# Layer 1 of a two-layer stream encoder: plain chunks by tile, column sums in two goes, paced stores

## The chip, the cores and the metric

The kernel runs on one core of one Trainium2 chip. The metric is the device time of one execution in microseconds. Before the change it is 2186.94 us (median of three runs, 2185.77 to 2187.29).

The engines named here are PE (TensorE, matrix products; PEld is its weight load), DVE (VectorE), ACT (ScalarE), POOL (GpSimd) and SP (SyncE, which issues most DMAs). All work from queues of their own, in order, and wait for each other on semaphores.

## The reference

A sequence of 1024 prompt frames and 32 sample frames, each of 1024 channels, goes through two layers. Cut to what matters here:

```python
for i in range(DEPTH):                       # DEPTH = 2
    mod = silu(c) @ w_ada[i] + b_ada[i]      # sh1, sc1, gt1, sh2, sc2, gt2
    h = rmsnorm(x, g_norm[i, 0]) * (1 + sc1) + sh1
    if i == 0:
        mix, v = sgu_mixer(h, ...)           # gated mixing in chunks of frames
    else:
        mix = pool_mixer(h_ext, ...)         # trailing means over 2, 4, 8, 16 frames, then a map per group
    x = x + gt1 * rmsnorm(mix, g_norm[i, 1])
    h = rmsnorm(x, g_norm[i, 2]) * (1 + sc2) + sh2
    f = square(relu(h @ ffn_w_up[i])) @ ffn_w_down[i]     # 1024 -> 4096 -> 1024
    x = x + gt2 * rmsnorm(f, g_norm[i, 3])
```

All of it is in float32. The change concerns layer 1 (`i = 1`): its FFN, the last line, and the order in which the pool mixer's work is done around it.

## The kernel before

**Tiles and chunks.** Frames are columns; they are cut into three tiles: tile 0 and tile 1 of 384 prompt frames each, tile 2 of 256 prompt and 32 sample frames (288 columns). The FFN's 4096 hidden channels are cut into eight chunks of 512. One chunk for one tile (a chunk-tile) is four up products (`ffn_item.up`, 8 x 3 matmuls each) and eight down products (`ffn_item.down`, 4 x 3 matmuls each), 192 matmuls. The factor 3 comes from splitting each float32 operand into a high and a low part in a format that PE multiplies at full rate: high by high, high by low, low by high. Tiles named with h and l (`hh`/`hl`, `fh`/`fl`, `wh`/`wl`) are these parts. A chunk's down products are put off (`pending`, `flush`) until the next chunk-tile's first up product has been issued.

**The passes.** The list `passes` (L321 to L328) says in which order chunks and tiles are taken. In layer 1: chunks 0 and 1 for tile 0, the same two for tile 1, then chunks 2 and 3 with each weight used for both tiles (chunk 3 with tile 1 first), then four "combined" chunks 4 to 7 (`COMBINED = 4`), then all eight chunks for tile 2.

**Combined chunks.** For chunks 4 to 7 the up products of tiles 0 and 1 are computed together (`combined_item`, L1554) by a scheme with seven block products in place of eight: blocks of the weights and of the two tiles' columns are added and subtracted beforehand. The weight side is made by `do_s` (L441) in a scratch area that lies in tile 2's `acc`. The column side is made by `sums_of_columns` (L1752), one "column" of four blocks at a time: three loads of tiles 0's and 1's modulated rows from DRAM (`md[0]`, `md[1]`), four subtractions on DVE, four high parts on ACT and four low parts on DVE. The results live in pieces of buffers that other work has left: the `hh`/`hl` rooms of tile 2, half of those of tile 1, two slots of the weight pool, and others. Before tile 2's rooms and `acc` can be used so, tile 2's modulated rows are stored to DRAM (`md[2]`); `late_modulation` (L1823) loads them again and makes tile 2's `hh` and `hl` at the last combined chunk.

**Weights.** `stream` lists all weight items in the order of their use, 512 KB each, eight to a chunk. SP loads an item into one of three `raw` buffers; `do_w` (L416) makes its high part on ACT and its low part on DVE, in two of 16 slots of the pool `W`. `stream_ready` (L620) limits the items in hand: eight before the position `wtight` (L371), and from there on 14 slots, which is seven items.

**Order of the work around the products.** Everything that isn't a product of the main sequence is a generator in the queue `fillers`: the residual and norm after a layer-0 FFN, the pool mixer and the modulation of layer 1 (`ffn1_0`, `ffn1_1`, `ffn1_2`, one for each tile, with `mix_to_ffn`, L1717), the column sums (`sums`), late modulation, and the output (`out_0`, `out_1`, `out_2`, from `to_out`, L2021). `weave` (L721) is called after each product. It prepares weight items, and pulls steps of the first two fillers while a running estimate of DVE's time is behind PE's. A filler's step may yield a number: that filler is then not pulled again for so many microseconds of the planner's time. `finish(tag)` (L732) pulls all that is left of a filler at once. Tile t's first layer-1 chunk calls `finish("ffn1_t")` (in `run_ffn`, L2003), and the last plain chunk-tile of tile 1 calls `finish("ffn1_2")` and only then starts the filler `sums` (L1548 to L1550). `run_ffn` calls `finish("sums")` ahead of each combined chunk.

**Output.** Tiles 0 and 1 end in `to_out`: a residual, then for each of eight groups of channels a transpose on DVE and four stores of that group, three from SP and one from POOL (L2084). Each group is one step that yields False.

Of the kernel before, what the change touches and what calls it, by code (L numbers as in the profile page):

```python
# [9 lines left out]
F32 = mybir.dt.float32  # L10
F32R = mybir.dt.float32r
AF = mybir.ActivationFunctionType
# [23 lines left out]
def tile_stream_encoder_step(  # L36
# [285 lines left out]
    passes += [(0, c, every) for c in range(2, 4)]  # L322
    passes += [(0, c, [t]) for t in every for c in range(4, 8)]
    pair = every[:-1]
    passes += [(1, c, [t]) for t in pair for c in (0, 1)]
    passes += [(1, c, pair if c != 7 - COMBINED else pair[::-1]) for c in range(2, 8)]
    combined = range(len(passes) - COMBINED, len(passes))
    passes += [(1, c, [NT - 1]) for c in range(8)]  # L328

# [103 lines left out]
    def temp(i):  # L433
        return scratch[:, 1024 + 384 * i : 1408 + 384 * i]
# [1064 lines left out]
    def ffn_item(p, t, after):  # L1499
        l, c, tiles = passes[p]  # L1500
        last = t == tiles[-1]
        n = ncol[t]
        hid = []

        def up(j):
            ps = ps_up(f"pf{l}_{c}_{t}_{j}")
            products(ps, n, up_terms(("up", p, j), t))
            if last:
                w_finish(("up", p, j))
            r = t_m(f"r{l}_{c}_{t}_{j}")  # L1510
            act(out=r[:, :n], in_=ps[:, :n], func=AF.Relu)  # L1511
            a, b = t_hid("h", f"fh{l}_{c}_{t}_{j}"), t_hid("l", f"fl{l}_{c}_{t}_{j}")
            act(out=r[:, :n], in_=r[:, :n], func=AF.Square)
            split(a, b, r, n)
            hid.append((a, b))

        def down():
            for d in range(KB):
                ps = ps_dn(f"pg{l}_{c}_{t}_{d}")
                wh, wl = need_w(("dn", p, d // 2))  # L1520
                terms = []
                for j in range(4):
                    o = j * 256 + (d % 2) * P
                    a, b = hid[j]
                    terms.append((wh[:, o : o + P], wl[:, o : o + P], a[:, :n], b[:, :n]))
                products(ps, n, terms)
                accumulate(t, d, ps, c == 0)
                if d == 0 and after is not None:
                    st = Stat(t, f"rf{l}_{t}", l == 0 or t < NT - 1)
                if after is not None:  # L1530
                    st.square(d)
                    if l == 1 and t == NT - 1:
                        scale_last(d)
                        if d in (2, 4, 6):
                            turn_last(d - 2)
# [12 lines left out]
        if p + 1 == combined[0] and t == 1:  # L1548
            finish("ffn1_2")
            fillers.append(("sums", sums_of_columns()))  # L1550
        pending.append(down)


    def combined_item(p, after):  # L1554
# [121 lines left out]
        weave()  # L1676
        for t in tiles:
            down(t)

    last_ps = {}  # L1680

# [35 lines left out]
    def mix_to_ffn(st, l):  # L1717
        t = st.t
        out = []
        need_ada(l, 2)  # L1720
        yield from residual(st, l, 1, f"r1_{l}_{t}", out)
        if l == 1 and t == NT - 1:
            for q in range(P // DEC):
                nc.sync.dma_start(xsd[:, :, q, :], acc[t][DEC * q : DEC * (q + 1), :, HALO:])
        need_ada(l, 4)
        if l == 0:
            yield from modulate(out[0], l, 2, 3)
            return
        got = []
        yield from out[0].finish(got)  # L1730
        if t < NT - 1:
            yield from apply(t, l, 2, 3, got[0])
            nc.sync.dma_start(md[t], acc[t][:, :, HALO:])
            return
        for k in range(KB):
            for c0, w, v in segs[t]:
                a = A(t, k, c0, w)
                stt(
                    out=a,
                    in0=a,  # L1740
                    scalar=coef[:, l, 2, v, k : k + 1],
                    in1=got[0][:, c0 : c0 + w],
                    op0=ALU.mult,
                    op1=ALU.mult,
                )
            yield False
        nc.sync.dma_start(md[t], acc[t][:, :, HALO:])
        yield False

    sums = {}  # L1750

    def sums_of_columns():  # L1752
        n = ncol[0]
        rooms = [room(part, NT - 1, f"sums_{part}", F32R) for part in "hl"]
        pieces = [
            r.rearrange("p k n -> p (k n)")[:, i * n : (i + 1) * n] for r in rooms for i in range(6)
        ]
        for name, tag, bufs, shape, k in (
            ("c", "c", 3, [P, 384], 1),
            ("r", "rr", 2, [P, 384], 1),  # L1760
            ("a", "aa", 2, [P, 512], 1),
            ("w", "W", W_SLOTS, [P, 1024], 2),
        ):
            for i in range(2 if tag == "W" else bufs):
                x = work.tile(shape, F32R, tag=tag, bufs=bufs, name=f"sums_{name}{i}")
# [9 lines left out]
        sums["spare"] = pieces  # L1775
        dsh = small.tile([P, 4], F32, tag="st", bufs=6, name="dshift")
        sh = shift[:, 1, 1, :, 0].rearrange("p (k a) -> p k a", a=2)
        tt(out=dsh, in0=sh[:, :, 1], in1=sh[:, :, 0], op=ALU.subtract)
        sums["parts"] = {}
        for i in range(4):  # L1780
            t1, t3, t2 = (temp(m) for m in range(3))
            t4 = t_m(f"sums_m{i}")
            nc.sync.dma_start(t1, md[0][:, 2 * i, :])
            nc.sync.dma_start(
                scratch[:, 1408:2176].rearrange("p (a n) -> p a n", a=2), md[1][:, 2 * i : 2 * i + 2, :]
            )
            nc.sync.dma_start(t4, md[0][:, 2 * i + 1, :])
            yield 3.0
            tt(out=t1, in0=t3, in1=t1, op=ALU.subtract)
            tt(out=t3, in0=t2, in1=t3, op=ALU.subtract)  # L1790
            tt(out=t2, in0=t2, in1=t1, op=ALU.subtract)
            tt(out=t4, in0=t4, in1=t2, op=ALU.subtract)
            yield True
            todo = (
                (2, t3, dsh[:, i : i + 1]),
                (0, t1, None),
                (1, t2, shift[:, 1, 1, 2 * i + 1, 0:1]),
                (3, t4, None),
            )
            for j, src, b in todo:  # L1800
                hi, lo = his.pop(0), los.pop(0)
                sums["parts"][j, i] = hi, lo
                if b is None:
                    act(out=hi, in_=src, func=AF.Copy)
                else:
                    act(out=hi, in_=src, func=AF.Identity, bias=b, scale=1.0)
            yield True
            for j, src, b in todo:
                hi, lo = sums["parts"][j, i]
                if b is None:  # L1810
                    tt(out=lo, in0=src, in1=hi.bitcast(F32), op=ALU.subtract)
                else:
                    stt(
                        out=lo,
                        in0=src,
                        scalar=b,
                        in1=hi.bitcast(F32),
                        op0=ALU.add,
                        op1=ALU.subtract,
                    )  # L1820
            yield False

    def late_modulation(t):  # L1823
        a = acc[t][:, :, HALO:]
# [196 lines left out]
    def to_out(st):  # L2021
# [48 lines left out]
        def run():  # L2070
# [9 lines left out]
            for k in range(KB):  # L2080
                time["dve"] += 0.1 + npr / 930.0
                nc.vector.transpose(out=turned[:, k, :], in_=A(t, k))
                for q in range(P // DEC):
# [4 lines left out]
                yield False  # L2088

        fillers.append((f"out_{t}", run()))  # L2090

# [47 lines left out]
```

## Time and profile before

| | |
|---|---|
| median of three runs | 2186.94 us |
| lowest and highest | 2185.77, 2187.29 us |
| profiled execution, its own time | 2187.31 us |
| profiled execution, span | 2185.4 us |
| mean granted PE clock over the span | 0.993 |
| DMA | 321.63 MB, mean 147 GB/s |

The span runs from the first instruction of the program to the last one's end; the execution's own time has 1.9 us around it. The profile comes from one execution. Its page has the busy time of each engine, slices of the span with a digit for the busy share, the chain of work that ended last, the costliest groups of instructions and the DMAs. Other views answer questions about a stretch: busy time of the engines in it, who waited for whom, groups of instructions by line, or the instructions in order of time. Names in these rows are the program's tile names without their numbers (`pf` is a PSUM tile of an up product, `pg` of a down product, `pn` of a norm, `pp` of the pool mixer's map). Matmuls overlap in the pipeline, so the mean duration of one is about twice the time from one to the next; the count in a stretch tells the rate. L80 is the helper through which nearly all DVE instructions are issued, so those are told apart by their tiles.

### The profile page before, as it was taken

How to read it: one execution, taken by the hardware profiler on the slowest of the kernel's cores; microseconds unless marked ns; L12 is line 12 of the kernel's file. 1: busy time of each engine (PE TensorE's matmuls, PEld its weight loads, DVE VectorE, ACT ScalarE, POOL GpSimd, SP SyncE). 2: the span in 40 equal slices, each digit the busy share in tenths (PEclk: the TensorE clock that was granted, in tenths of full speed). 3: DMA queues.
4: the chain of work that ended last, by engine and by line, in shares of the span. 5: the costliest groups of instructions: out<-in, count | busy, mean ns of one | idle time of the engine just before them, and what ended most of it. 6: DMA issues, size and time to landing. Idle time of an engine off the chain costs nothing.

```text
span 2185.4 us, 33239 instructions
## 1 busy us (share of the span) xinstructions
PE 2141.9 (98%) x13137; PEld 2063.5 (94%) x13137; DVE 1491.8 (68%) x2649; ACT 1000.0 (46%) x1716; POOL 15.4 (1%) x34
## 2 busy tenths in 40 slices
PE   9999999999999999999999999987999999999998
PEld 6778999999999999999999999977999999999998
DVE  6777738567787549567887778775666555577664
ACT  5534331233465552314346466655444443355454
POOL 0000000000000000000000000000000000001000
PEclk9999999999999999999999999998999999999999
DMA  8486524353356444335665566564343222156771
GB/s 303 145 261 211 167 80 134 96 161 115 112 152 200 126 147 142 107 97 172 180 183 158 154 185 201 164 190 134 105 123 119 78 68 68 49 152 172 208 205 62
DMA packets 380849, 321.63 MB, mean 147 GB/s; under 512 B 39730, under 2 KB 343386, under 8 KB 380692
## 3 DMA queue, kind: packets, MB, share of 16 engines
q1 hardware_dynamic: 380020, 318.61, 48.0%
q8 instruction: 103, 1.69, 0.3%
q0 software_dynamic: 640, 0.88, 0.1%
q14 instruction: 54, 0.44, 0.1%
q10 hardware_dynamic: 32, 0.01, 0.0%
HBM read 283.28 MB, written 36.17 MB: 146 GB/s over the span
## 4 chain that ended last, share of the span: by engine, by line
PE 89%; DVE 5%; DMA 3%; ACT 2%; issue 1%; DVEq 0%; ACTq 0%
PE pg L923 10%; PE pg L925 10%; PE pg L924 10%; PE pf L923 8%; PE pf L924 8%; PE pf L925 8%; PE po L923 3%; PE po L924 3%; PE po L925 3%; PE pu L923 3%; PE pu L925 3%; PE pu L924 3%; PE pv L951 2%; PE pv L950 2%; PE pv L952 2%; PE pf_0a L1588 2%
## 5 line engine op out<-in xcount | busy, mean ns | idle before, releaser
L923 PE MATMUL pg<-fh,wh_dn 128*128 128x384 f32 (+1 forms) x1440 | 463.6, 322 | 1.4 <-ACT fh L1336 1.0
L924 PE MATMUL pg<-fl,wh_dn 128*128 128x384 f32 (+1 forms) x1440 | 461.0, 320 | 2.1 <-DVE fl L80 1.9
L925 PE MATMUL pg<-fh,wl_dn 128*128 128x384 f32 (+1 forms) x1440 | 460.2, 320 | 2.3 <-DVE wl_dn L80 2.3
L923 PE MATMUL pf<-hh,wh_up 128*128 128x384 f32 (+1 forms) x1280 | 409.7, 321 | 3.4 <-ACT r L1511 1.7
L924 PE MATMUL pf<-hl,wh_up 128*128 128x384 f32 (+1 forms) x1280 | 408.2, 319 | 0.8 <-DVE hl L80 0.8
L925 PE MATMUL pf<-hh,wl_up 128*128 128x384 f32 (+1 forms) x1280 | 408.0, 319 | 0.1
L923 PEld LDWEIGHTS pg<-fh,wh_dn 128*128 128x128 f32 x1440 | 270.1, 188 | 5.2 <-ACT fh L1336 3.0
L924 PEld LDWEIGHTS pg<-fl,wh_dn 128*128 128x128 f32 x1440 | 270.3, 188 | 4.0 <-DVE fl L80 3.4
L925 PEld LDWEIGHTS pg<-fh,wl_dn 128*128 128x128 f32 x1440 | 270.1, 188 | 2.8 <-DVE wl_dn L80 2.8
L80 DVE TENSOR_TENSOR wl_up<-raw,wh_up 128x1024 fp32r<-128x1024 f32 (+1 forms) x160 | 177.1, 1114 | 131.6 <-ACT wh_up L419 130.7
L80 DVE TENSOR_TENSOR acc<-acc,pg 128x384 f32<-128x384 f32 (+1 forms) x336 | 172.3, 516 | 107.1 <-PE pg L925 106.3
L923 PEld LDWEIGHTS pf<-hh,wh_up 128*128 128x128 f32 x1280 | 240.6, 188 | 5.0 <-ACT r L1511 2.3
L924 PEld LDWEIGHTS pf<-hl,wh_up 128*128 128x128 f32 x1280 | 240.8, 188 | 2.0 <-DVE hl L80 1.5
L925 PEld LDWEIGHTS pf<-hh,wl_up 128*128 128x128 f32 x1280 | 241.2, 188 | 1.0 <-DVE wl_up L80 1.0
L419 ACT ACTIVATE wh_up<-raw 128x1024 fp32r<-128x1024 f32 x136 | 143.8, 1059 | 204.5 <-PE pf L924 118.7
L80 DVE TENSOR_TENSOR wl_dn<-raw,wh_dn 128x1024 fp32r<-128x1024 f32 x152 | 185.4, 1221 | 73.6 <-ACT wh_dn L419 63.9
L419 ACT ACTIVATE wh_dn<-raw 128x1024 fp32r<-128x1024 f32 x152 | 160.5, 1058 | 158.5 <-PE pg L924 117.0
L80 DVE SCALAR_TENSOR_TENSOR aa<-raw,csil,aa 128x512 f32<-128x512 f32 (+1 forms) x364 | 203.1, 618 | 6.9 <-DMA raw<-in_w_ada_dram 6.9
L1511 ACT ACTIVATE r<-pf 128x384 f32<-128x384 f32 (+1 forms) x160 | 71.3, 447 | 172.4 <-PE pf L925 144.2
L923 PE MATMUL pu<-hh,wh_u 128*128 128x384 f32 (+1 forms) x384 | 125.8, 328 | 0.0
L923 PE MATMUL po<-ush,wh_o 128*128 128x384 f32 (+1 forms) x384 | 123.5, 322 | 0.0
L925 PE MATMUL pu<-hh,wl_u 128*128 128x384 f32 (+1 forms) x384 | 123.4, 321 | 0.0
(509 smaller groups left out, 3546.6 us busy)
## 6 DMA issues: line engine op xcount, KB each, us to landing
raw<-in_ffn_w_up_dram SPq DMA_DIRECT2D x152, 512.0 KB, 4.0
raw<-in_ffn_w_down_dram SPq DMA_DIRECT2D x152, 512.0 KB, 3.5
raw<-in_w_ada_dram SPq DMA_DIRECT2D x96, 512.0 KB, 4.4
raw<-in_sgu_w_in_dram SPq DMA_DIRECT2D x40, 512.0 KB, 4.3
xd<-acc SPq DMA_DIRECT2D x8, 1536.0 KB, 7.2
raw<-in_sgu_w_out_dram SPq DMA_DIRECT2D x24, 512.0 KB, 3.7
xo_r<-xd SPq DMA_DIRECT2D x32, 384.0 KB, 4.0
vd<-vt SPq DMA_DIRECT2D x32, 256.0 KB, 4.7
```

The costliest lines, as they stand in the source:

```text
L80: return op(out, *args, **kw)
L419: act(out=wh, in_=r, func=AF.Copy)
L923: mm(ps[:, :n], wh, rh, start=i == 0, stop=False)
L924: mm(ps[:, :n], wh, rl, start=False, stop=False)
L925: mm(ps[:, :n], wl, rh, start=False, stop=i == last)
L950: mm(ps[:m, :], a_h, wh[:, o : o + 512], start=k == 0, stop=False)
L951: mm(ps[:m, :], a_h, wl[:, o : o + 512], start=False, stop=False)
L952: mm(ps[:m, :], a_l, wh[:, o : o + 512], start=False, stop=k == KB - 1)
L1511: act(out=r[:, :n], in_=ps[:, :n], func=AF.Relu)
L1588: mm(ps[:, :n], u, v, start=first and k == 0 and x == 0, stop=k == 3 and x == 2, skip_group_check=True,)
```

## The change

1. The passes of layer 1: chunks 0 to 3 for tile 0 alone, then chunks 0 to 3 for tile 1 alone, then the four combined chunks. Chunks 2 and 3 no longer share their weights between the tiles, so their 16 items are loaded and split twice.
2. `wtight` is 24 items ahead of the first combined item and no longer 8.
3. The column sums are made in two goes. Three of the four columns follow directly on tile 2's modulation, inside the filler `ffn1_2`, with two high parts of each column in spare pieces. The fourth (`other_sums`) is started where all four were started before; it uses tile 1's rooms, and then copies the six high parts from the spare pieces into tile 1's rooms. `finish("sums")` stands behind the first two products of a combined chunk.
4. In the last combined chunk `finish("ffn1_2")` (late modulation) is called after each tile's down products.
5. Each step of the output of tiles 0 and 1 yields 5.0 in place of False.

```diff
@@ passes
-    passes += [(1, c, [t]) for t in pair for c in (0, 1)]
-    passes += [(1, c, pair if c != 7 - COMBINED else pair[::-1]) for c in range(2, 8)]
+    passes += [(1, c, [t]) for t in pair for c in range(8 - COMBINED)]
+    passes += [(1, c, pair) for c in range(8 - COMBINED, 8)]
@@ weights
-    wtight = min(wpos[s[1]] for s in stream if s[0] == "s") - 8
+    wtight = min(wpos[s[1]] for s in stream if s[0] == "s") - 24
@@ ffn_item
         if p + 1 == combined[0] and t == 1:
             finish("ffn1_2")
-            fillers.append(("sums", sums_of_columns()))
+            fillers.append(("sums", other_sums()))
@@ combined_item
         flush()
         next(first)
         next(first)
+        finish("sums")
         next(first)
...
         for t in tiles:
             down(t)
+            if after is not None:
+                finish("ffn1_2")
@@ mix_to_ffn
         nc.sync.dma_start(md[t], acc[t][:, :, HALO:])
         yield False
+        yield from sums_of_columns()
@@ sums_of_columns
-        his = [hh[1][:, 2 * i, :] for i in range(4)] + [hl[1][:, 2 * i, :] for i in range(4)]
-        his += [pieces.pop(0) for _ in range(8)]
-        los = [pieces.pop() for _ in range(16)]
+        sums["his"] = [pieces.pop(0) for _ in range(8)]
+        sums["los"] = [pieces.pop() for _ in range(16)]
         sums["spare"] = pieces
...
-        for i in range(4):
+        sums["dsh"] = dsh
+        for i in range(3):
+            yield from sum_columns(i, sums["spare"][2 * i : 2 * i + 2])
+
+    def other_sums():
+        homes = [(hh[1][:, 2 * i, :], hl[1][:, 2 * i, :]) for i in range(4)]
+        yield from sum_columns(3, homes[3])
+        for i in range(3):
+            for j, home in zip((0, 2), homes[i]):
+                hi, lo = sums["parts"][j, i]
+                act(out=home, in_=hi.bitcast(F32), func=AF.Copy)
+                sums["parts"][j, i] = home, lo
+            yield True
+        yield False
+
+    def sum_columns(i, homes):
+        n = ncol[0]
+        dsh = sums["dsh"]
+        home = {0: homes[0], 2: homes[1]}
+        t1, t3, t2 = (temp(m) for m in range(3))
+        t4 = t_m(f"sums_m{i}")
...
         for j, src, b in todo:
-                hi, lo = his.pop(0), los.pop(0)
+            hi, lo = home[j] if j in home else sums["his"].pop(0), sums["los"].pop(0)
@@ run_ffn
             if p in combined:
-                finish("sums")
                 combined_item(p, after if c == 7 else None)
@@ to_out
                         turned[DEC * q : DEC * (q + 1), k, :].rearrange("p (b c) -> p b c", c=DEC),
                     )
-                yield False
+                yield 5.0
```

More of the change, by code (lines that the diff above doesn't have):

```diff
@@ L1748, in mix_to_ffn @@
         yield False
+        yield from sums_of_columns()
     sums = {}
     def sums_of_columns():
+        assert not any(f[0] in ("ffn1_0", "ffn1_1") for f in fillers)
         n = ncol[0]
@@ L1771, in sums_of_columns @@
         pieces.append(wide.rearrange("p a b -> p (a b)")[:, :n])
-        his = [hh[1][:, 2 * i, :] for i in range(4)] + [hl[1][:, 2 * i, :] for i in range(4)]
-        his += [pieces.pop(0) for _ in range(8)]
-        los = [pieces.pop() for _ in range(16)]
+        sums["his"] = [pieces.pop(0) for _ in range(8)]
+        sums["los"] = [pieces.pop() for _ in range(16)]
         sums["spare"] = pieces
+        sums["parts"] = {}
         dsh = small.tile([P, 4], F32, tag="st", bufs=6, name="dshift")
@@ L1778, in sums_of_columns @@
         tt(out=dsh, in0=sh[:, :, 1], in1=sh[:, :, 0], op=ALU.subtract)
-        sums["parts"] = {}
-        for i in range(4):
[L1781 to L1792, printed above, removed]
-            yield True
[L1794 to L1800, printed above, removed]
-                hi, lo = his.pop(0), los.pop(0)
[L1802 to L1820, printed above, removed]
-            yield False
@@ new lines, in sum_columns @@
+    def sum_columns(i, homes):
[4 more added lines that the diff above has]
+        t4 = t_m(f"sums_m{i}")
+        nc.sync.dma_start(t1, md[0][:, 2 * i, :])
+        nc.sync.dma_start(
+            scratch[:, 1408:2176].rearrange("p (a n) -> p a n", a=2), md[1][:, 2 * i : 2 * i + 2, :]
+        )
+        nc.sync.dma_start(t4, md[0][:, 2 * i + 1, :])
+        yield 3.0
+        tt(out=t1, in0=t3, in1=t1, op=ALU.subtract)
+        tt(out=t3, in0=t2, in1=t3, op=ALU.subtract)
+        tt(out=t2, in0=t2, in1=t1, op=ALU.subtract)
+        tt(out=t4, in0=t4, in1=t2, op=ALU.subtract)
+        yield True
+        todo = (
+            (2, t3, dsh[:, i : i + 1]),
+            (0, t1, None),
+            (1, t2, shift[:, 1, 1, 2 * i + 1, 0:1]),
+            (3, t4, None),
+        )
+        for j, src, b in todo:
+            hi, lo = home[j] if j in home else sums["his"].pop(0), sums["los"].pop(0)
+            sums["parts"][j, i] = hi, lo
+            if b is None:
+                act(out=hi, in_=src, func=AF.Copy)
+            else:
+                act(out=hi, in_=src, func=AF.Identity, bias=b, scale=1.0)
+        yield True
+        for j, src, b in todo:
+            hi, lo = sums["parts"][j, i]
+            if b is None:
+                tt(out=lo, in0=src, in1=hi.bitcast(F32), op=ALU.subtract)
+            else:
+                stt(
+                    out=lo,
+                    in0=src,
+                    scalar=b,
+                    in1=hi.bitcast(F32),
+                    op0=ALU.add,
+                    op1=ALU.subtract,
+                )
+        yield False
@@ L2087, in run @@
                     )
-                yield False
+                yield 5.0
         fillers.append((f"out_{t}", run()))
```

## The prediction

> **What bounds the kernel now.** I read the page first (span, busy shares, slices), then a table of stretches cut where one kind of work ends, then the waits of PE, and last the order of time of DVE and SP where a step is moved.
>
> ```profile
> span 2185.4 us, 33239 instructions
> PE 2141.9 (98%) x13137; PEld 2063.5 (94%) x13137; DVE 1491.8 (68%) x2649; ACT 1000.0 (46%) x1716; POOL 15.4 (1%) x34
> ...
> PE   9999999999999999999999999987999999999998
> ...
> PEclk9999999999999999999999999998999999999999
> ```
>
> PE is busy for 98% of the span, so no more than 43.5 us (2185.4 - 2141.9) of it is idle, and in only two neighbouring slices (54.6 us each, about 1420 to 1530) does that show. The stretches cut there are layer 1's plain chunks, the gap between them, the summed chunks (from 1705.3) and tile 2 (from 1957.5). Columns: length, then busy us of PE, PEld, DVE, ACT and POOL, granted clock, DMA share, GB/s.
>
> ```profile
> 1300.00:1391.00 91.00, 90.57 (x674) 90.16 (x673) 75.46 (x118) 56.32 (x92) 0.00 (x0) 1.00 0.72 221
> 1391.00:1465.50 74.50, 73.63 (x397) 68.94 (x396) 59.49 (x93) 45.66 (x78) 0.00 (x0) 1.00 0.55 169
> 1465.50:1490.30 24.80, 4.57 (x16) 2.57 (x14) 17.02 (x28) 9.47 (x17) 0.00 (x0) 0.55 0.35 120
> 1490.30:1495.50 5.20, 5.19 (x15) 4.75 (x16) 5.20 (x11) 2.69 (x5) 0.00 (x0) 0.50 0.00 0
> 1495.50:1705.30 209.80, 208.67 (x1191) 205.19 (x1191) 131.21 (x256) 95.86 (x177) 0.00 (x0) 1.00 0.39 118
> ...
> 1957.50:2176.00 218.50, 211.52 (x1571) 208.28 (x1570) 140.56 (x217) 110.42 (x187) 9.98 (x16) 1.00 0.58 160
> ```
>
> Between 1465.5 and 1490.3 PE runs 16 matmuls where it has room for some 140 (at 0.175 us each, worked out below). In the next 5.2 us it is busy, but at half clock. The other stretches hardly idle: 1.1 us of 209.8 in the plain chunks, 7.0 us of 218.5 in tile 2. The waits of PE from 1391 to 1710 name the gap:
>
> ```profile
> PE pn_r_1x L816 <- ACT sc_r_1x L801: 15.0, 1, 15.0
> PE pn_rp L816 <- ACT sc_rp L801: 2.8, 1, 2.8
> PE pf L923 <- ACT hh L896: 1.3, 1, 1.3
> ...
> PE pg L924 <- DVE fl L80: 1.0, 2, 0.8
> PE pg L923 <- ACT fh L1336: 0.6, 1, 0.6
> ```
>
> These are tile 1's norms (pn) and the modulated rows (hh) of its FFN. At its first layer-1 chunk the code forces out all that is left of tile 1's mixer (finish("ffn1_1") in run_ffn), and PE has nothing else in its order. Tile 0 had two chunks, 1391 to 1465.5, to cover that work; it wasn't enough.
>
> **The change, part by part.** The sum is made against the profiled execution's own 2187.31 us (1.9 more than its span); it lies 0.37 above the median of 2186.94.
>
> *Tile 0's chunks 2 and 3 ahead of tile 1* (the passes). PE's matmuls stay the same in number: eight chunk-tiles of 192 each, then the summed ones. A matmul at full clock takes 208.67/1191 = 0.175 us, a chunk-tile 33.6 us. Tile 1 is now due 67.3 us later. The gap of 24.8 us shrinks to what its 16 matmuls need, 16 x 0.175 = 2.8: a gain of **22.0**. With no long idle before them, the 15 matmuls at half clock take 2.6 instead of 5.2: a gain of **2.6**. What hides tile 1's rest: DVE's part of it is 17.02 + 5.20 us and 2.2 more (two each of hl and acc,r_r_1x after 1495.5), 24.4 in all. A chunk-tile's own DVE work comes from these groups of the plain stretch (count | busy, mean ns | idle before):
>
> ```profile
> L80 DVE TENSOR_TENSOR acc<-acc,pg 128x384 f32<-128x384 f32 x39 | 21.4, 548 | 7.9 <-PE pg L925 7.9
> L80 DVE TENSOR_TENSOR wl_up<-raw,wh_up 128x1024 fp32r<-128x1024 f32 (+2 forms) x18 | 17.5, 986 | 21.6 <-ACT wh_up L419 21.6
> L80 DVE TENSOR_TENSOR wl_dn<-raw,wh_dn 128x1024 fp32r<-128x1024 f32 x12 | 14.6, 1219 | 10.8 <-ACT wh_dn L419 10.8
> L80 DVE TENSOR_TENSOR fl<-r,fh 128x384 fp32r<-128x384 f32 x24 | 13.3, 556 | 10.4 <-ACT fh L1336 10.1
> ...
> L80 DVE TENSOR_TENSOR acc<-acc 128x384 f32<-128x384 f32 x12 | 6.7, 556 | 8.5 <-DMA acc<-md 8.4
> ...
> L80 DVE TENSOR_TENSOR sl_up<-acc,sh_up 128x1024 fp32r<-128x1024 f32 x3 | 3.7, 1223 | 1.8 <-PE pg L924 1.8
> ...
> L80 DVE SCALAR_TENSOR_TENSOR hl<-acc,shift,hh 128x384 fp32r<-128x384 f32 x2 | 1.1, 616 | 0.2 <-ACT hh L896 0.2
> L80 DVE SCALAR_TENSOR_TENSOR acc<-acc,coef,r_r_1x 128x384 f32<-128x384 f32 x2 | 1.1, 615 | 0.0
> ```
>
> Eight weight splits of 1.22, eight accumulations of 0.548 and four fl of 0.556 make 16.4 us. Two chunk-tiles leave 67.3 - 32.8 = 34.5 us for the 24.4: it fits, though its chain of two norms has to be threaded through. If that fails, the rest is late at tile 1's first chunk: 0 to 8 us (a third of the work), I take **+1.0**, since only its last rows would be late and PE starts on the first. PE's own small stops under such a load: 0.43 us in the 91 before, 0.87 in the 74.5; I take **+1.0**, bounds 0 and 5.
>
> *Sixteen more weight items.* Chunks 2 and 3 are now read twice: 16 loads of 512 KB, 16 copies on ACT (1.06 each, 17.0 us) and 16 splits on DVE (19.5 us). No matmul is added, so they cost nothing while the engines have room. DVE from 1465.5 to the summed chunks: 17.02 + 5.20 + 131.21 + 19.5 = 172.9 us in 239.8 - 24.6 = 215.2, 80% busy. It held 83% from 1300 to 1391 and 80% from 1391 to 1465.5, with PE fed. ACT: (9.47 + 2.69 + 95.86 + 17.0)/215.2 = 58%. The loads add 8.4 MB, 39 GB/s over 215.2 us, to the 118; from 1300 to 1391 the chip moved 221 GB/s with PE idle for 0.43 us. The limit on items in hand (seven instead of eight over the last 24 plain items) leaves seven times 33.6/8 = 4.2 us of lead, 29 us. **0.**
>
> ```profile
> L419 ACT ACTIVATE wh_dn<-raw 128x1024 fp32r<-128x1024 f32 x12 | 12.7, 1061 | 28.4 <-PE pg L924 26.8 <-PE pf L924 1.6
> ...
> L1804 ACT ACTIVATE sums_h<-acc 128x384 fp32r<-128x384 f32 x2 | 1.0, 518 | 4.4 <-DVE acc L80 4.4
> ```
>
> *Column sums in two goes.* Three columns now follow tile 2's modulation at once; the fourth and six copies on ACT (0.52 each, 3.1 us) come after tile 1's last ups, and the first summed chunk needs them from its third product. SP shows the columns' pace:
>
> ```profile
> 1640.89 0.56 SPq L1747 DMA_DIRECT2D md<-acc  x1
> ...
> 1647.76 0.34 SPq L1783 DMA_DIRECT2D acc<-md  x1
> ...
> 1676.20 0.32 SPq L1783 DMA_DIRECT2D acc<-md  x1
> ```
>
> Four columns start 1647.76 to 1676.20, so one takes 9.5 us, of it 8 x 0.556 = 4.4 on DVE. The first load waits on SP 6.9 us for the store of tile 2's rows, as now; the weight loads queued behind it have their 29 us of lead. The cover for the fourth column is the last plain down (96 matmuls) and two products of 12: 120 x 0.175 = 21.0 us. DVE has in that time eight accumulations (4.4), the column (4.4) and the four summed weight items. One of those is about 4.0 (sl_up 1.22, four quarter differences, two low parts: 2.8 by their sizes, an estimate from the rows above): 24.8 in all, though two of the items are due a little later. I take **+3.0**, because some of the three early columns may be left over as well. Bounds: -1.6 (the fl and fh waits above vanish), and 4 x 9.5 - 21.0 = 17 if no column was early.
>
> *Tile 2's late modulation* is forced behind the first last down. In PE's waits from 1900 to 2180, and in DVE's order of time:
>
> ```profile
> PE pg L925 <- DVE wl_dn L80: 2.3, 2, 1.2
> PE pn_rf L816 <- ACT sc_rf L801: 1.5, 1, 1.5
> PE pf L923 <- ACT r L1511: 1.4, 1, 1.4
> ...
> PE pf L924 <- DVE hl L80: 0.8, 1, 0.8
> ...
> PE pf L923 <- ACT wh_up L419: 0.4, 1, 0.4
> ```
>
> ```profile
> 1959.28 4.55 DVE L80 SCALAR_TENSOR_TENSOR hl<-acc,shift,hh 128x256 fp32r<-128x256 f32 x16
> 1963.75 0.55 DVE L80 TENSOR_TENSOR acc<-acc,pg 128x384 f32<-128x384 f32 x1
> ```
>
> Tile 2's first chunk waits for hl 0.8 us. Forced earlier, the block of 4.55 us stands ahead of the second down's accumulations, and those waits (PE through three PSUM buffers) are late instead. **-1.0**, bounds -2.2 (0.8 and the 1.4) and +4.6.
>
> *Stores paced.* The output rows of tiles 0 and 1 go out 5 us apart a row group instead of in bursts, which hold weight loads on the same queue:
>
> ```profile
> 1984.17 7.29 SPq L2084 DMA_DIRECT2D out_dram<-turned  x12
> 1991.56 0.42 SPq L411 DMA_DIRECT2D raw<-in_ffn_w_up_dram  x1
> ```
>
> A weight load stands 7.3 us behind twelve stores. PE's weight waits in tile 2 sum to 2.3 + 0.4 + 1.4 = 4.1. Eight groups of 5 us, two tiles, end long before 2176. **-1.5**, bounds -4.1 and +3 (the same bytes spread over more weight loads).
>
> Sum: 2187.31 - 22.0 - 2.6 + 1.0 + 1.0 + 3.0 - 1.0 - 1.5 = 2165.2; less the 0.37, **2164.8**.
>
> The clock's row is 0.55 over the gap, so it fell about 2.5 us after 1465.5, and it stayed at 0.50 for 5.2 us of matmuls. [...]
>
> **Rivals.** (a) *The stop moves to the first summed chunk.* If two of the three early columns are left over, three columns, 28.5 us, stand against 21.0: 7.5 us of idle plus the half clock's 2.6, in place of 3.0: **2172**. For it: tile 2's chain took from 1495.5 to 1640.9 with DVE at 62%, and must now share with 19.5 us more. Against: it gets two chunk-tiles' time that tile 1's rest doesn't fill.
> (b) *No change.* If fillers are held back during tile 0's chunks 2 and 3, the 24.4 us are forced at tile 1 as before: **2187**. Against: DVE did 59.49 us in 74.5 in the chunks just before.
> (c) *Slower: DVE becomes the bound of the plain chunks.* If it can't be used beyond the 131.21/209.8 = 62.5% of that stretch now, 172.9 us of work take 276.6, 36.8 more than the 239.8 of today: **2224**. It decides below 72% (172.9/239.8). For it: its idle time there is spent behind ACT's copies (21.6 and 10.8 us). Against: ACT itself waits there for PE to free weight buffers (26.8 us), which is slack, and DVE held 80 to 83% before.
>
> **How the numbers follow.** Forecast 0.69, (a) 0.20, (b) 0.04, (c) 0.07. The likeliest case alone spans 2154 (all lower bounds) to about 2171, where the stops at tile 1 and at the summed chunks are twice as long and the last two steps gain nothing; (a) with more left over reaches 2178. All lower bounds at once are unlikely, so the range is **2155 to 2178**. 0.2% is 4.4 us, about what a measurement here can tell: faster 0.89, same 0.04, slower 0.07.
>
> **What would show it.** Right: no stretch near 1465 with PE under half busy and no clock below 1 between 1391 and the summed chunks; those start about 1683; DVE near 80% in the plain stretch; wait for sc_r_1x gone. (a) shows as a PE wait on sums parts and a clock of 0.5 there. (c) shows as many PE waits for wl_up, wl_dn and fl. I am wrong on the main step if pn_r_1x still waits over 5 us, and on the last two if tile 2's stretch idles more than 7.0 us.

## The result, and the profile after

| | before | changed |
|---|---|---|
| median of four runs each, same chip | 2186.36 us | **2156.44 us** |
| lowest and highest | 2185.04, 2187.29 us | 2155.18, 2157.30 us |
| ratio, 95% interval | | 0.9863 (0.9846 to 0.9880) |
| profiled execution, its own time | 2187.31 us | 2157.29 us |
| profiled execution, span | 2185.4 us | 2155.4 us |

The changed kernel is 29.9 us faster; 22.1 us faster were forecast (2186.94 to 2164.8), and the time lies near the lower end of the range. The page of the changed kernel, at the same places as before:

```profile
span 2155.4 us, 33342 instructions
PE 2134.9 (99%) x13137; PEld 2060.1 (96%) x13137; DVE 1508.5 (70%) x2665; ACT 1016.6 (47%) x1738; POOL 15.3 (1%) x34
...
PE   9999999999999999999999999999999999999998
...
PEclk9999999999999999999999999999999999999999
```

PE has the same 13137 matmuls and no slice below 9 any more but the last. 7.0 us of its busy time went (2141.9 to 2134.9): 3.1 between layer 1's first product and the summed chunks, where 9 matmuls run at half clock in place of 29, 1.9 in tile 2, and 2.1 ahead of layer 1, which the change doesn't touch. Its idle time fell from 43.5 to 20.5 us. DVE has 16 instructions more and ACT 22, the second making of 16 weight items and six copies of column sums; they are busy for 16.7 and 16.6 us more.

The table of stretches, with the columns of before. The old gap, 1465.5 to 1490.3, comes first; then everything from its start to the first summed chunk (1681.6), a small piece of that, the summed chunks, and tile 2.

```profile
1465.50:1490.30 24.80, 24.80 (x142) 23.52 (x141) 21.60 (x41) 19.02 (x37) 0.00 (x0) 1.00 0.41 129
...
1465.50:1681.60 216.10, 213.27 (x1202) 207.13 (x1201) 169.53 (x308) 123.21 (x216) 0.00 (x0) 0.99 0.55 168
...
1560.00:1570.00 10.00, 8.05 (x33) 6.69 (x32) 1.75 (x3) 3.12 (x8) 0.00 (x0) 0.83 0.66 201
...
1681.60:1935.40 253.80, 252.75 (x1445) 250.02 (x1444) 141.44 (x246) 115.88 (x214) 0.00 (x0) 1.00 0.28 84
1935.40:2145.60 210.20, 207.58 (x1556) 205.96 (x1556) 139.22 (x214) 109.87 (x186) 9.95 (x16) 1.00 0.61 166
```

Where 16 matmuls ran in 24.8 us, 142 run now, at full clock. DVE does 169.53 us in 216.1, or 78%, with PE fed; 80% were expected. The summed chunks are as long as before. Tile 2 is shorter than it was: 210.2 us against 218.5 from about the same cuts (before, 2.2 of those lie outside its products; from its first up product to its last down product it is 216.5 against 210.2).

The waits of PE from 1391 to 1690, and from there to 2160:

```profile
PE pp L2015 <- DMA wg<-in_pool_w_grp_dram: 1.9, 1, 1.9
PE pg L924 <- DVE fl L80: 0.7, 1, 0.7
...
PE pn_rf L816 <- ACT sc_rf L801: 1.5, 1, 1.5
PE pg L923 <- ACT sums_l L1336: 0.9, 1, 0.9
PE pf L924 <- DVE hl L80: 0.8, 1, 0.8
PE pf L923 <- ACT r L1511: 0.2, 1, 0.2
```

The wait of 15.0 us for sc_r_1x is gone, and so are those for sc_rp and hh. No wait stands at the first summed chunk. A new one has come in: PE waits 1.9 us for the weights of tile 2's pool map (wg), in the piece 1560 to 1570, where the clock is 0.83. Tile 2's waits for wl_dn and wh_up are gone; those for sc_rf and hl stand as they were.

Cut where layer 1's products start and where each kind ends, the 30.0 us between the two profiled executions are:

| stretch | before | changed | difference | forecast |
|---|---|---|---|---|
| up to layer 1's first up product | 1374.3 | 1372.8 | -1.5 | 0 |
| from there to the first summed chunk | 330.9 | 308.9 | -22.0 | -22.6 |
| summed chunks | 253.6 | 253.8 | +0.1 | +3.0 |
| tile 2, to its last down product | 216.5 | 210.2 | -6.3 | -2.5 |
| end | 10.2 | 9.8 | -0.4 | 0 |

The forecast's stop of 3.0 us for the sums stands behind the first two products of the first summed chunk, and its 1.0 for late modulation at tile 2's first product. The first row is no effect of the change. Layer 1 starts between 1372.6 and 1374.4 in the profiles of all kernels here, most of which are the same up to that point.

### The profile page after: what moved, and what is told of

It reads as the page before. It is cut to its first block, busy times and chain, and to the rows that moved or that the text cites. A ratio compares the mean times of both kernels' runs of the same rounds, so it can differ in the third digit from the quotient of the medians.

```text
span 2155.4 us, 33342 instructions
## 1 busy us (share of the span) xinstructions
PE 2134.9 (99%) x13137; PEld 2060.1 (96%) x13137; DVE 1508.5 (70%) x2665; ACT 1016.6 (47%) x1738; POOL 15.3 (1%) x34
## 4 chain that ended last, share of the span: by engine, by line
PE 87%; DVE 5%; DMA 4%; ACT 2%; issue 1%; SPq 0%; DVEq 0%; ACTq 0%
PE pg L923 10%; PE pg L925 10%; PE pg L924 10%; PE pf L923 8%; PE pf L924 8%; PE pf L925 8%; PE po L923 3%; PE po L925 3%; PE po L924 3%; PE pu L923 3%; PE pu L925 3%; PE pu L924 3%; PE pv L951 2%; PE pv L950 2%; PE pv L952 2%; PE pf_0a L1588 2%
## 5 line engine op out<-in xcount | busy, mean ns | idle before, releaser
L80 DVE TENSOR_TENSOR wl_up<-raw,wh_up 128x1024 fp32r<-128x1024 f32 (+1 forms) x168 | 186.6, 1119 | 105.0 <-ACT wh_up L419 104.3
L419 ACT ACTIVATE wh_up<-raw 128x1024 fp32r<-128x1024 f32 x144 | 152.2, 1058 | 191.3 <-PE pf L924 118.7
L419 ACT ACTIVATE wh_dn<-raw 128x1024 fp32r<-128x1024 f32 x160 | 169.0, 1058 | 152.8 <-PE pg L924 101.9
L80 DVE TENSOR_TENSOR wl_dn<-raw,wh_dn 128x1024 fp32r<-128x1024 f32 x160 | 195.4, 1222 | 58.2 <-ACT wh_dn L419 48.8
L1511 ACT ACTIVATE r<-pf 128x384 f32<-128x384 f32 (+1 forms) x160 | 71.3, 446 | 176.6 <-PE pf L925 174.0
```

What stands on the lines that cost most here:

```text
L80: return op(out, *args, **kw)
L419: act(out=wh, in_=r, func=AF.Copy)
```

## The experiments

Each kernel was timed four times (pacing alone eight times) beside the kernel before, on one chip; the numbers of kernels from different rounds of timing are compared by their distance to the kernel before of that round. Differences of 1 to 2 us between rounds are not read.

### Passes alone, pacing alone, all but pacing

The first three take the change apart. One kernel is the kernel before with the pacing only, one is the kernel before with the new passes only (the four columns then all start behind tile 1's last up products), and one is the changed kernel without the pacing.

```diff
@@ e1_pace_only, against the kernel before
-                yield False
+                yield 5.0
@@ e2_passes_only, against the kernel before
-    passes += [(1, c, [t]) for t in pair for c in (0, 1)]
-    passes += [(1, c, pair if c != 7 - COMBINED else pair[::-1]) for c in range(2, 8)]
+    passes += [(1, c, [t]) for t in pair for c in range(8 - COMBINED)]
+    passes += [(1, c, pair) for c in range(8 - COMBINED, 8)]
@@ e3_after_no_pace, against the changed kernel
-                yield 5.0
+                yield False
```

Pacing alone:

> The kernel before with one part of the change: each output step of tiles 0 and 1 yields 5.0. Theory (pacing is what emptied tile 2's stretch of waits, 7.0 us of PE idle before, about 1 after): 5 to 6 us less than before, 2180 to 2182, with the gap of 24.8 us at tile 1 still there and the clock at 0.5 over it. Rival (tile 2's waits went because the work before it was ordered otherwise): within 1 us of before, 2185.5 to 2187.5.

The passes alone:

> The kernel before with one part of the change: the order of passes (four plain chunks of tile 0, then four of tile 1). All four columns of sums are then started after tile 1's last ups. Theory: the gap at tile 1 goes (24.6 us), and four columns at 9.5 us, 38 us, stand against 21 us of cover at the first summed chunk, a new stop of 10 to 17 us plus up to 2.6 for the half clock: 2172 to 2181, 5 to 14 less than before. Rival (the second go isn't needed, the sums hide anyway): 22 to 24 less than before, 2162 to 2164.

All but the pacing:

> The changed kernel with the output steps yielding False again. Theory (pacing is worth 5 to 6 us): 2161.5 to 2162.5 against 2156.4, with weight waits back in tile 2's stretch. Rival (pacing is worth little once the order is changed): 2155.5 to 2157.5.

| | time | against before | ratio, 95% |
|---|---|---|---|
| pacing alone | 2181.80 | -5.2 | 0.9972 (0.9962 to 0.9982) |
| passes alone | 2165.28 | -21.7 | 0.9899 (0.9886 to 0.9913) |
| all but pacing | 2162.25 | -24.7 | 0.9882 (0.9867 to 0.9897) |

The pacing is worth 5 to 6 us with or without the rest, several times the 1.5 forecast. The passes alone bring 21.7. The long stop at the first summed chunk that was expected of them did not come. PE's waits of that kernel from 1391 to 1720:

```profile
PE pf_0a L1588 <- ACT sums_l L1806: 2.1, 1, 2.1
PE pp L1993 <- DMA wg<-in_pool_w_grp_dram: 1.1, 1, 1.1
```

and the first load of each of its four columns in SP's order of time:

```profile
1630.06 0.34 SPq L1783 DMA_DIRECT2D acc<-md  x1
...
1660.91 0.34 SPq L1783 DMA_DIRECT2D acc<-md  x1
...
1671.64 0.32 SPq L1783 DMA_DIRECT2D acc<-md  x1
...
1678.69 0.32 SPq L1783 DMA_DIRECT2D acc<-md  x1
```

The first column's loads come 30 us ahead of the others' even in one go, and its first subtractions on DVE run from 1636; the others' loads come 7 to 11 us apart instead of 9.5 each. So part of the columns' time lies ahead of the cover of 21 us. PE's order helps too: seven matmuls of the next product, which need only the first three columns, stand ahead of the first matmul that needs the last one. The stop is 2.1 us where 10 to 17 were expected; how much of that each of these is worth isn't shown.

### Parts of the change that might do nothing

One kernel has the changed one's finish("ffn1_2") behind the last downs taken out (late modulation). Another has the passes and the pacing only: no second go of the sums, no late modulation, wtight at 8.

```diff
@@ e5_no_late, against the changed kernel
-            if after is not None:
+            if False:
                 finish("ffn1_2")
```

> The changed kernel without the call that forces late modulation behind the last downs. Theory (the block of 16 hl stands at the same place with and without it, as the profile of the changed kernel shows it right behind tile 2's first matmuls again): no difference, 2155 to 2158, the wait on hl still 0.8 us. Rival (the prediction's step, the call gains 1.0): 2157 to 2158.5 and a longer wait on hl.

> The kernel before with two parts of the change: the order of passes and the pacing of stores. Theory (these two are nearly all of it; the second go of the sums saves the 2.1 us wait on the sums that the order of passes alone showed): 2158 to 2160.5. Rival (the two goes are worth nothing, as their copies and earlier loads cost what they save): 2155.5 to 2157.5.

Without late modulation's call: 2158.69, 29.4 below before; ratio 0.9865 (0.9851 to 0.9880). Its instructions stand in the same order on every engine as the changed kernel's, so the call changes nothing, and this run is also a second measurement of the changed kernel, in another round.

What holds tile 2's hl is a buffer. `sums_of_columns` takes the rooms of tile 2 for its pieces (`sums_h`, `sums_l`), and in the last summed chunk tile 1's hidden parts lie in `sums_l`, which is the room that hl needs. In the changed kernel's order of time PE's last matmul that reads it, and DVE's block of hl:

```profile
1935.21 0.33 PE L925 MATMUL pg<-sums_l,wl_dn 128*128 128x384 f32 x1
...
1935.90 4.55 DVE L80 SCALAR_TENSOR_TENSOR hl<-acc,shift,hh 128x256 fp32r<-128x256 f32 x16
```

The block starts 0.36 us after that matmul's end. By the code it can't start before it, wherever the generator is pulled.

Passes and pacing only: 2158.93, 29.1 below before, ratio 0.9865 (0.9851 to 0.9880). **Two parts of the change, the order of passes and the pacing, hold all of its gain.** The sums in two goes save a stop of 2.4 us there; their wait for wg was 1.9 us in place of 1.3.

PE's waits of the kernel with passes and pacing only, from 1391 to 1700, and the engines around the first of them:

```profile
PE pf_0a L1588 <- ACT sums_l L1806: 2.4, 1, 2.4
PE pp L1993 <- DMA wg<-in_pool_w_grp_dram: 1.3, 1, 1.3
...
1680.00:1695.00 15.00, 12.56 (x63) 11.97 (x62) 14.12 (x29) 7.08 (x14) 0.00 (x0) 0.89 0.35 110
```

### How much cover tile 1's rest needs

Three plain chunks for each of tiles 0 and 1, and the fourth shared with its weights made once:

```diff
@@ e4_three_ahead, against the changed kernel
-    passes += [(1, c, [t]) for t in pair for c in range(8 - COMBINED)]
-    passes += [(1, c, pair) for c in range(8 - COMBINED, 8)]
+    passes += [(1, c, [t]) for t in pair for c in range(7 - COMBINED)]
+    passes += [(1, c, pair) for c in range(7 - COMBINED, 8)]
```

> The changed kernel with three plain chunks for tile 0, three for tile 1, and the fourth for both (tile 0 first), so tile 1 is due 33.6 us earlier than in the changed kernel and eight weight items fewer are loaded. Theory (tile 1's rest needs the time of two chunk-tiles; in the changed kernel its last hl ends at about 1530, and tile 1 would be due at about 1498): 8 to 12 us of stop at tile 1 with the half clock, 2164 to 2171. Rival (one more chunk of cover is enough, as the engines have room): 2155 to 2158.

2162.54 (2159.79 to 2167.49), 24.4 below before, so some 5 us of the gain are lost; the direction is as expected and the size below it. PE's waits from 1391 to 1690, and the engines around tile 1's first chunk, which is due 33.6 us earlier than in the changed kernel:

```profile
PE stT_p L1946 <- ACT acc L1923: 2.9, 1, 2.9
PE pf L923 <- ACT hh L896: 1.3, 1, 1.3
...
1490.00:1510.00 20.00, 15.76 (x84) 14.45 (x83) 19.39 (x33) 9.30 (x14) 0.00 (x0) 0.91 0.73 229
```

The first row stands at transposes of tile 2's pool state, which come first in PE's order here. Tile 1's first hh is not done before 1504.4, when the stop ends, so its products would have waited as long without them: tile 1's rest is late by 4.2 us with three chunks. DVE is busy for 19.39 of these 20 us. With four chunks there is no such wait. The 16 weight items are cheaper than the stop that they remove, and one chunk fewer is not enough. The profile shows only part of the loss: it is of the fastest of the four executions, 2.7 us below the median, with a granted clock of 0.998 over the span, and the other three had 0.996 to 0.997.

### The new wait for the pool map's weights

In the changed kernel the map's weights are asked for and multiplied within one step of tile 2's filler. This kernel puts 4 us of the planner's time between the load and the products. A second one also lets the residual of the output wait 4 us behind its step (`yield 4.0 if t > 0 else False`), for the 1.5 us at sc_rf.

```diff
@@ e7_early_wg, against the changed kernel (mixer of layer 1)
                 nc.sync.dma_start(wg, pool_w_grp[0, g].rearrange("(k p) d -> p k d", p=P))
+                if t == NT - 1 and g == 0:
+                    yield 4.0
```

> The changed kernel with 4.0 us of the planner's time between the load of tile 2's first pool weights and the matmuls that use them. Theory (PE's wait on that load, 1.95 us, and the 3.4 us at half clock behind it are what is left in the plain chunks): 2 to 3.5 us less, 2153 to 2154.5, no clock below 1 there. Rival (the load's lateness is a chance of one execution, or the gate makes another step late): 2155.5 to 2157.5.

> As the one before, and the output of tile 1 starts 4.0 us of the planner's time later, so that its norm's matmuls don't stand ahead of tile 2's products before their input is ready. Theory: the wait of pn_rf on sc_rf, 1.5 us, goes as well: 2151.5 to 2153. Rival (PE's place for these matmuls is chosen elsewhere): as the one before.

2155.41 (2154.57 to 2156.70) and 2155.93 (2153.69 to 2157.56), where the changed kernel's order took 2158.69 in the same round. So the wait for wg and what follows it cost about 3 us there. Part of this is a matter of the execution: the kernels with False, 1.0, 2.0 and without stores have the same order of work up to tile 2, and in their profiles the same wait is 1.0 to 1.5 us long and the clock stays at 1.00. The second kernel's extra wait at the residual does nothing: sc_rf still holds PE for 1.5 us. Of the first, the engines in the piece that was at 0.83, and PE's waits from 1391 to 1700:

```profile
1560.00:1570.00 10.00, 10.00 (x56) 9.58 (x55) 3.46 (x7) 5.59 (x10) 0.00 (x0) 1.00 0.84 244
...
PE pg L923 <- ACT fh L1336: 2.1, 1, 2.1
...
```

The piece is full and at full clock. A wait of 2.1 us has come elsewhere, without a drop of the clock.

### A smaller change

The kernel before with the passes, the pacing, and those two lines for wg; the sums in one go as they always were.

> The order of passes, the pacing and the earlier load of the pool weights, with the sums in one go as before the change. Theory (the second go is worth the 2.4 us wait on the sums and a half-clock window behind it, once no other stop lies ahead): 2 to 4 us over e7_early_wg's 2155.4, 2157.4 to 2159.4. Rival (the sums' second go is worth nothing either way): 2154.5 to 2156.5.

**2154.76 (2154.31 to 2154.87)**, 32.5 below before; ratio 0.9849 (0.9832 to 0.9865). With the sums in two goes and the same lines for wg (the kernel of the section before) the distance was 32.6, so the two goes are worth nothing once the passes give the sums room. This is the lowest median of the kernels that do the whole computation. The changed kernel lay 29.9 and 29.4 below before in its two rounds. The smaller change's largest wait of PE from 1391 to 1700 is the sums' own:

```profile
PE pf_0a L1588 <- ACT sums_l L1806: 1.7, 1, 1.7
...
```

### What pacing does

The working theory here was that the stores themselves cost nothing, and that pacing only moves ACT's copies and DVE's splits of weights to better places among the output's work. Two kernels yield 1.0 and 2.0 instead of 5.0.

> The changed kernel with output steps that yield 1.0 in place of 5.0. A group's three stores take about 1.6 us to issue on SP, and a weight item is due every 3.1 us in tile 2. Theory (what costs is a weight load's place on SP behind many stores, not the bytes): at 1.0 us the stores still fill the queue ahead of the loads, so most of the 6 us comes back: 2160 to 2163 on the scale of the changed kernel's 2156.4 to 2158.7. Rival (any gate is enough, since it lets weight items be pulled in between): 2156 to 2158.7.

> The changed kernel with output steps that yield 2.0. Theory: stores take 1.6 us of each 2.0 on SP while one tile is written and more while both are, so part of the waits comes back: 2157.5 to 2161. Rival (any gate is enough): 2156 to 2158.7.

The last kernel is the changed one without pacing, in which the stores are left out altogether.

```diff
@@ e12_no_store, against e3_after_no_pace
-                for q in range(P // DEC):
-                    (nc.gpsimd if q == 3 else nc.sync).dma_start(
-                        dst[q, k],
-                        turned[DEC * q : DEC * (q + 1), k, :].rearrange("p (b c) -> p b c", c=DEC),
-                    )
                 yield False
```

> The changed kernel without the pacing (yield False again in to_out), and with the eight groups of output stores of tiles 0 and 1 left out, so that the rows of tiles 0 and 1 are not written; the transposes and the residual stay. With pacing and stores the kernel took 2156.4 us, without pacing 2162.3. Theory (what pacing changes is where ACT's copies and DVE's splits of the weights stand among the output work in the two engines' orders, so that raw buffers come free late; the stores on the SP queue and their bytes are not it): 2160 to 2163, and DVE's splits of the items that land 33 to 44 us into tile 2 still stand about 10 us behind their copies. Rival (the prediction's mechanism: weight loads stand behind bursts of twelve stores on SP, or share bandwidth with them): 2155.5 to 2158, as with pacing.

| step of the output yields | time | against before |
|---|---|---|
| nothing (False) | 2162.25 | -24.7 |
| 1.0 | 2162.92 | -24.3 |
| 2.0 | 2165.48 | -21.7 |
| 5.0 (the changed kernel) | 2156.44 | -29.9 |
| nothing, and no stores | 2155.27 | -30.9 |

Without the stores the time is that of the paced kernel (ratio 0.9856, 0.9840 to 0.9873), as the rival had it: **the working theory fell**. The dose does not go one way: 2.0 is worse than nothing. SP's order of time in the kernel without pacing, the first twenty us of the output of tile 0:

```profile
1957.25 0.40 SPq L411 DMA_DIRECT2D raw<-in_ffn_w_down_dram  x1
1957.69 2.69 SPq L2105 DMA_DIRECT2D out_dram<-turned  x4
1960.47 0.45 SPq L411 DMA_DIRECT2D raw<-in_ffn_w_up_dram  x1
1960.96 7.37 SPq L2105 DMA_DIRECT2D out_dram<-turned  x12
1968.43 0.43 SPq L411 DMA_DIRECT2D raw<-in_ffn_w_up_dram  x1
1968.90 3.90 SPq L2105 DMA_DIRECT2D out_dram<-turned  x6
1972.91 2.06 SPq L411 DMA_DIRECT2D raw<-in_ffn_w_up_dram  x2
```

and the splits on DVE of the same kernel that free the three raw buffers, each the buffer of the third load after its own, with what follows:

```profile
1961.89 1.18 DVE L80 TENSOR_TENSOR wl_dn<-raw,wh_dn 128x1024 fp32r<-128x1024 f32 x1
1964.97 1.23 DVE L80 TENSOR_TENSOR wl_dn<-raw,wh_dn 128x1024 fp32r<-128x1024 f32 x1 [1.89 <-ACT wh_dn L419]
...
1985.25 1.22 DVE L80 TENSOR_TENSOR wl_up<-raw,wh_up 128x1024 fp32r<-128x1024 f32 x1
1986.46 0.46 DVE L80 TENSOR_TENSOR acc<-acc,pg 128x288 f32<-128x288 f32 x1
1988.04 0.45 DVE L80 TENSOR_TENSOR acc<-acc,pg 128x288 f32<-128x288 f32 x1 [1.12 <-PE pg L925]
...
1993.15 2.36 DVE L80 TENSOR_TENSOR wl_up<-raw,wh_up 128x1024 fp32r<-128x1024 f32 x2
```

A buffer is free at 1963.1 (1961.89 + 1.18), but its load leaves at 1968.43, behind twelve stores: 5.4 us late. The next is free at 1966.2 and leaves at 1972.91: 6.7 us late. The splits of the items loaded so then stand behind accumulations that wait for PE, the second and third from 1993.15 on, about 10 us after ACT's copies (2.94 us for three of them, from 1981.40).

In the changed kernel and in the one with 2.0, SP looks like this:

```profile
1960.36 0.40 SPq L411 DMA_DIRECT2D raw<-in_ffn_w_up_dram  x1
1960.80 0.58 SPq L2105 DMA_DIRECT2D out_dram<-turned  x1
1963.33 0.40 SPq L411 DMA_DIRECT2D raw<-in_ffn_w_up_dram  x1
```

```profile
1988.06 0.42 SPq L411 DMA_DIRECT2D raw<-in_ffn_w_up_dram  x1
1988.52 4.25 SPq L2105 DMA_DIRECT2D out_dram<-turned  x6
1992.87 1.33 SPq L411 DMA_DIRECT2D raw<-in_ffn_w_up_dram  x1
...
```

At 5.0 at most three stores stand between two loads, and no load of tile 2 leaves more than 1.0 us after its buffer is free. At 2.0 they come six at a time, later in tile 2, and loads leave up to 4.9 us late. Without stores none is late. The stretch of tile 2 follows. It is 216.4 to 217.7 us with False and 2.0, 215.4 with 1.0, and 209.1 to 211.1 us in every kernel with 5.0 and in the one without stores. The table of stretches of the unpaced kernel and of the one without stores, for tile 2:

```profile
1935.20:2151.90 216.70, 209.92 (x1557) 206.32 (x1556) 138.94 (x214) 109.79 (x186) 9.95 (x16) 1.00 0.59 161
```

```profile
1934.70:2144.00 209.30, 207.00 (x1559) 206.12 (x1558) 140.20 (x214) 110.86 (x186) 0.00 (x0) 1.00 0.52 152
```

One thing these runs don't separate. ACT's and DVE's orders are fixed when the program is built, with the stores in the plan. Leaving the stores out changed them too: but for the split that stands behind tile 2's block of hl, none is more than 1.2 us behind its copy. So it is shown that the loss needs the stores, and that bunches of them hold loads on SP. That late loads alone make the loss is not shown, and two kernels side by side speak against it. In the one with 1.0 and in the second kernel of the wg section, which has 5.0, up to six stores stand between two loads and loads leave up to 2.4 us late, four of them over 1 us in each. Tile 2 takes 215.4 us in the first and 209.7 in the second. What goes with the loss is the latest split on DVE. It stands 9.9, 8.8 and 8.8 us behind its copy with False, 1.0 and 2.0, and 6.4 us at most in the kernels with 5.0. That is no proof that late splits are the cause, and why 2.0 is worse than nothing stays open. The stores' bytes are not it: the paced kernel stores as many.

## Why the prediction was right, and where it was off

**The gap of 24.8 us** (-22.0 and -2.6): right. Two chunk-tiles more ahead of tile 1 remove it, and the passes alone measured -21.7. Of the two added costs, +1.0 for tile 1's last rows was 0, with no wait for sc_r_1x or hh left. Of the +1.0 for small stops under the load there was more than thought, but of another kind: 213.27 busy of 216.1 is 2.8 us of idle, 1.9 of it at wg, and the half clock behind it cost 1.7 more. No step of the prediction named that load. That the stretch still came within 0.6 us of its forecast (-22.0 for -22.6) is partly luck: one cost didn't come and an unnamed one did.

**Sixteen more items at nothing**: right, with the cover that was named. DVE is 78% busy in the stretch and PE waits for none of the split weights in it. Rival (c), DVE bound at 62.5%, is out. Nor is the spare large: with one chunk less as cover DVE fills 19.39 of 20 us and PE waits.

**Sums in two goes** (+3.0): mis-sized; 0 in the profile of the changed kernel, where PE does not wait at the first summed chunk. The step took DVE as the place where the columns would pile up, and costed their pace at 9.5 us; the first three columns' loads leave SP at 1631 to 1645 and the fourth's at 1657, 25 us ahead of the first summed chunk (1681.6), and no wait is left. Rival (a) did not come. Stops of 1.7 to 2.4 us are what one go costs.

**Late modulation** (-1.0): wrong. The step took finish("ffn1_2") behind the downs for an earlier start of the block of hl. The order of instructions is the same with and without the call, and hl holds PE for the same 0.8 us. Its room is read by tile 1's down products until 1935.54, and the block starts at 1935.90. That could have been seen from the code, by following which buffers the last summed chunk still uses.

**Stores paced** (-1.5): right in direction, mis-sized: -5.2 (24.7 and 29.9 below before), and -6.3 in the profile. Of its mechanism, bursts that hold weight loads, the holding is shown; that this is what costs the time is not. The working took the listed weight waits of PE, 4.1 us, as the upper bound of the gain, and less than half of it as the value. 1.4 of these are a wait for ACT's r (L1511), no weight wait, and count in late modulation's bound as well. And the bound was wrong. Between the unpaced and the paced kernel, PE's idle time in tile 2 falls by 4.2 us (216.70 - 209.92 = 6.8 to 2.6), and the busy time of the same products by 2.3 more (209.92 to 207.58, 1557 and 1556 matmuls). That part shows in no wait, since PE counts as busy: a matmul lasts 0.29 us there and the next can start 0.13 us behind it, so a short delay doesn't show as idle.

**The sum.** The stretches missed by -1.5, +0.6, -2.9, -3.8 and -0.4: -8.0. The -3.8 in tile 2 is -4.8 for the pacing and +1.0 for late modulation; the -2.9 is the stop at the sums that did not come. With the 0.5 by which the changed profiled execution lies further above its median (2157.29 against 2156.44) that is the 8.4 us between 2164.8 and 2156.4. What was said to show the result came as said, except the clock, which did drop once ahead of the summed chunks (0.50 for 3.42 us), and the start of those chunks, 1681.6 for about 1683.

## What to carry to other kernels

When PE is the bound and stops at one place, buy it time with work that it has to do anyway, even at the price of loading weights twice, as long as DVE and ACT keep some room in that stretch (DVE was busy for 78% of it here and ACT for 57%, with no wait of PE for split weights). Where bursts of stores share a queue with the loads that feed the bound, try spacing them out, measure more than one spacing (5.0 gained 5.2 us here, 1.0 and 2.0 nothing), look at the order of the other engines as well as at the queue, and don't take the listed waits for the whole loss. And take a change of several parts apart: here two parts brought all of the gain, one did nothing at all, and the two with an earlier load were the fastest version.

## What was not expected of the hardware

Some short stops cost the clock in these kernels, and others did not. In the changed kernel PE's order of time shows the wait for wg, and the columns of the stretches what came behind it:

```profile
1563.99 3.83 PE L2015 MATMUL pp<-acc,wg 128*128 128x288 f32 x8 [1.95 <-DMA wg<-in_pool_w_grp_dram]
...
1564.36:1567.78 3.42, 3.42 (x9) 2.42 (x8) 0.00 (x0) 0.85 (x2) 0.00 (x0) 0.50 0.55 168
```

PE was idle for 1.95 us, and 3.42 us at half clock followed. About as much follows the 2.4 us stop with passes and pacing only (0.89 of 15 us, 3.3) and the late rows of the three-chunk kernel (0.91 of 20 us, 3.6). But waits of 2.1, 2.1 and 1.7 us in three other kernels (the passes alone, the earlier load of wg, the smaller change) left the clock at 1.00. So a stop of 2 us cost between 2 and about 3.7 us here (half of 3.4 on top). The prediction gave 2.6 us for the half clock behind a stop; it was 1.7 or nothing.

The length of the stop does not tell these cases apart: the clock was halved behind 1.95 us and not behind 2.1 us. What decides between them is not shown.
